# Expert rounds of 1792 columns in place of 896, in a two-layer hybrid decoder kernel

## The chip, the cores and the metric

The kernel runs on one NeuronCore of a Trainium2 chip. The metric is device time in microseconds (us) from launch to end, the median of several executions. TensorE (PE) multiplies, VectorE (DVE) and ScalarE (ACT) do the elementwise work, GpSimd (POOL) small index work, and SyncE (SP) issues nearly all transfers from device memory.

## The reference

The program is a two-layer decoder trunk on 256 tokens of width 1024, in float32. The part that the change touches is the last one, the expert feed-forward of the second layer:

```python
def moe_swiglu(h, router, we_gate, we_up, we_down):
    logits = (h @ router).astype(jnp.float32)
    top_v, top_i = lax.top_k(logits, TOP_K)
    top_w = jax.nn.softmax(top_v, axis=-1)
    gates = jnp.sum(jax.nn.one_hot(top_i, N_EXPERTS, dtype=jnp.float32) * top_w[..., None], axis=-2)
    gates = gates.astype(h.dtype)
    out = jnp.zeros_like(h)
    for e in range(N_EXPERTS):
        out = out + gates[..., e:e + 1] * swiglu(h, we_gate[e], we_up[e], we_down[e])
    return out
```

There are 8 experts, each token goes to 2 of them, and an expert's matrices are 1024x3584 (gate and up) and 3584x1024 (down): 44 MB an expert, 352 MB in all.

## The kernel before

Ahead of the experts stand the convolution layer, a dense feed-forward and the attention layer. They take the first 470 us or so and the change leaves their instructions as they are.

The experts are taken in an order that is worked out on the chip: those with more than 64 tokens alternate with the others, which keeps heavy and light experts next to each other. An expert's first 64 tokens go through `gate_up` and `down`. Up to 32 more, the overflow, go through `gate_up_over` and `down_over`, each inside an If on the register `over` (`over_parts`), so that PE jumps over them in an expert without overflow.

An expert is cut into `NR` rounds of `RW` columns of the hidden width; before, there are 4 rounds of 896. In a round PE does, in an order written out by hand (the loop over `rounds`, under `manual_schedule` for PE): `gate_up` of the first four blocks of 128 input rows; the transposes of the hidden values of the round before (`hidden_T`); if an expert has just ended, its `scatter` (the product with the tokens' placement matrix, which DVE then weighs and adds to `h`); in an expert's last round the `gather` of the next expert's tokens; overflow; `gate_up` of the other four blocks; overflow; and the seven `down` blocks of the round behind it. ACT and DVE make the hidden values from PSUM (`hidden`, `hidden_over`) while PE does those downs.

PSUM has eight banks of 512 columns. Before, `pa` and `pb` hold gate (upper 64 partitions) and up (lower 64), `po` the overflow, `py0` and `py1` the expert's output, and the three others turn (`bank`) among transposes, gather and scatter. The scatter splits the output into two float32r parts, `yh` and `yl`, and makes two products for each quarter of `h`.

Weights come through a ring of 19 tiles (`RING`, `raw_tile`) that SP fills in the order of use (`units`, `fetch`); SP issues a load when the readers of the tile 19 places earlier are done.

Of the kernel before, what the change touches and what calls it, by code (L numbers as in the profile page):

```python
# [17 lines left out]
P = 128  # L18
S = 256
# [28 lines left out]
def hybrid_kernel(  # L48
# [118 lines left out]
    with ExitStack() as ph:  # L167
# [189 lines left out]
        rows1 = consts.tile([P, P], F32, name="rows1")  # L357
# [303 lines left out]
    with ExitStack() as ph:  # L661
# [21 lines left out]
        def unit(v, src, how="(k p) n -> p k n"):  # L683
            sp.dma_start(v, src.rearrange(how, p=P))
            return v
# [11 lines left out]
        def units():  # L697

            for i in range(len(rounds) + 1):
                if i < len(rounds):  # L700
                    e, p = rounds[i]
                    for q in range(4):
                        for w in (sw_we_gate, sw_we_up):
                            t = raw_tile()[:, :2 * RW].rearrange("p (k n) -> p k n", k=2)
                            yield unit(t, matrix(w, e)[q * 256:(q + 1) * 256, p * RW:(p + 1) * RW])
                if i:
                    e, p = rounds[i - 1]
                    for q in range(4):
                        n = min(2, BLK - 2 * q)
                        t = raw_tile()[:, :n * D].rearrange("p (k n) -> p k n", k=n)  # L710
                        r0 = p * RW + 2 * q * P

                        yield unit(t, matrix(sw_we_down, e)[r0:r0 + n * P, :], "(p k) n -> p k n")
# [105 lines left out]
        pt = psm.enter_context(tc.tile_pool(name="pt", bufs=3, space=PSUM, reuse_waits="tile"))  # L819
        mwk = ga.enter_context(tc.tile_pool(name="mwk2", bufs=1, reuse_waits="tile"))  # L820

        def bank(name):
            return pt.tile([P, 512], F32, name=name, tag="t")

        def fixed(name):
            return pfix.tile([P, 512], F32, name=name)

        pa, pb, po = fixed("pa"), fixed("pb"), fixed("po")
        py = [fixed(f"py{n}") for n in range(2)]

# [70 lines left out]
        def gather(e, Pm):  # L901

            xe = wk.tile([P, KD, SL], F32, name="xe", tag="xe")
            for kk in range(2):
                b = bank("ga")[:, :4 * SL].rearrange("p (k n) -> p k n", k=4)
# [6 lines left out]
            b = bank("pmt")  # L912
# [3 lines left out]
            PT = wk.tile([P, 2, S], F32R, name="PT", tag="PT")  # L916
# [3 lines left out]
        def gate_up(xe, w, ks):  # L920
            for k in ks:
                x = xe[:, k, 0:HD]
                g, u = [v[:, k % 2, :] for v in w[2 * (k // 2):2 * (k // 2) + 2]]
                for ps, c0, c1 in ((pa, 0, A), (pb, A, RW)):
                    for half, v in ((0, g), (1, u)):
                        pe.matmul(ps[half * HD:(half + 1) * HD, :c1 - c0], x, v[:, c0:c1], start=(k == 0),  # L926
                                  stop=(k == KD - 1), tile_position=(0, half * HD))

        def gate_up_over(xe, w, ks):
            for k in ks:  # L930
                x = xe[:, k, HD:SL]
                for half, v in enumerate(w[2 * (k // 2):2 * (k // 2) + 2]):
                    for q, c0, c1 in ((2 * half, 0, A), (2 * half + 1, A, RW)):
                        pe.matmul(po[q * 32:(q + 1) * 32, :c1 - c0], x, v[:, k % 2, c0:c1], start=(k == 0),  # L934
                                  stop=(k == KD - 1), tile_position=(0, q * 32))

        def hidden():

            s = mwk.tile([P, A], F32, name="s", tag="s")
            hx = mwk.tile([P, A], F32, name="hx", tag="hx")  # L940
            act.activation(s[:HD, :], pa[:HD, :], AF.Silu)  # L941
            dve.tensor_tensor(hx[:HD, :], s[:HD, :], pa[HD:, :], op=OP.mult)  # L942
            act.activation(s[HD:, :B], pb[:HD, :B], AF.Silu)
            dve.tensor_tensor(hx[HD:, :2 * P], s[HD:, :2 * P], pb[HD:, :2 * P], op=OP.mult)
            dve.tensor_tensor(hx[HD:, 2 * P::2], s[HD:, 2 * P:B], pb[HD:, 2 * P:B], op=OP.mult)
# [7 lines left out]
        def hidden_over():  # L953
            s = mwk.tile([P, A], F32, name="so", tag="so")
            hx = mwk.tile([HD, A], F32, name="hxo", tag="hxo")
            act.activation(s[HD:, :B], po[:HD, :B], AF.Silu)
            act.activation(s[HD:HD + 32, B:], po[:32, B:], AF.Silu)  # L957
            dve.tensor_tensor(hx[:, :2 * P], s[HD:, :2 * P], po[HD:, :2 * P], op=OP.mult)  # L958
            dve.tensor_tensor(hx[:32, 2 * P:], s[HD:HD + 32, 2 * P:], po[HD:HD + 32, 2 * P:], op=OP.mult)
            dve.tensor_tensor(hx[32:, 2 * P::2], s[HD + 32:, 2 * P:B], po[HD + 32:, 2 * P:B], op=OP.mult)  # L960
            return hx

        def hidden_T(hx, hxo):
            b = bank("ht")
            for j in range(3):
                pe.transpose(b[:, j * P:(j + 1) * P], hx[:, hidden_block(j)], ident)
            pe.transpose(b[:, 3 * P:3 * P + HD], hx[:HD, hidden_block(3)], ident[:HD, :HD])  # L967
            hT = mwk.tile([P, 3 * P + HD], F32, name="hT", tag="hT")
            act.copy(hT, b[:, :3 * P + HD])  # L969
            b = bank("hto")  # L970
            for j in range(3):
                pe.transpose(b[:, j * HD:(j + 1) * HD], hxo[:, hidden_block(j)], ident[:HD, :HD])
            pe.transpose(b[:, 3 * HD:3 * HD + 32], hxo[:32, hidden_block(3)], ident[:32, :32])  # L973
            hTo = mwk.tile([P, 3 * HD + 32], F32, name="hTo", tag="hTo")
            dve.tensor_copy(hTo, b[:, :3 * HD + 32])  # L975
            return hT, hTo

        def down(p, hT, w):
            for q in range(BLK):
                o = q * P if q < 4 else (q - 4) * P + HD  # L980
                for n in range(2):
                    pe.matmul(py[n][n * HD:(n + 1) * HD, :], hT[:, o:o + HD], w[q // 2][:, q % 2, n * 512:(n + 1) * 512],  # L982
                              start=(p == 0 and q == 0), stop=(p == NR - 1 and q == BLK - 1),
                              tile_position=(0, n * HD))

        def down_over(p, hTo, w):
            for q in range(BLK):
                o = q * HD if q < 4 else (q - 4) * HD + 32
                i = p * BLK + q
                for n in range(2):  # L990
                    r = (HD, 0)[n] + 32 * (i % 2)
                    pe.matmul(py[n][r:r + 32, :], hTo[:, o:o + 32], w[q // 2][:, q % 2, n * 512:(n + 1) * 512],  # L992
                              start=(i < 2), stop=(i >= NR * BLK - 2), tile_position=(0, r))

        def outputs():
            ys = []
            for n in range(2):
                yh = mwk.tile([P, 512], F32R, name="yh", tag=f"yh{n}", bufs=1)
                yl = mwk.tile([P, 512], F32R, name="yl", tag=f"yl{n}", bufs=1)
                act.copy(yh, py[n])  # L1000
                dve.tensor_tensor(yl, py[n], yh.bitcast(F32), op=OP.subtract)  # L1001
                ys.append((yh, yl))
            return ys
# [167 lines left out]
```

## Time and profile before

| what | value |
|---|---|
| median of 3 runs | 1351.79 us (1348.92 to 1353.38) |
| profiled execution, its own time | 1349.67 us |
| its span, first to last instruction | 1348.0 us |
| PE busy, share of the span | 1282.6 us, 95% |
| DVE, ACT, POOL busy | 385.7, 298.9, 86.2 us |
| moved by the transfer queues | 420.91 MB, mean 312 GB/s |
| mean granted PE clock | 0.983 of full |

The profiled execution lies 2.1 us under the median of the runs, and 1.7 us of its time lie outside the span. A busy PE row means that matmuls follow each other; how close that is to the engine's best is seen from the spacing of their starts.

### The profile page before, as it was taken

How to read it: one execution, taken by the hardware profiler on the slowest of the kernel's cores; microseconds unless marked ns; L12 is line 12 of the kernel's file. 1: busy time of each engine (PE TensorE's matmuls, PEld its weight loads, DVE VectorE, ACT ScalarE, POOL GpSimd, SP SyncE). 2: the span in 40 equal slices, each digit the busy share in tenths (PEclk: the TensorE clock that was granted, in tenths of full speed). 3: DMA queues.
4: the chain of work that ended last, by engine and by line, in shares of the span. 5: the costliest groups of instructions: out<-in, count | busy, mean ns of one | idle time of the engine just before them, and what ended most of it. 6: DMA issues, size and time to landing. Idle time of an engine off the chain costs nothing. (4 is left out here: it accounts for less than half of the span.)

```text
span 1348.0 us, 19743 instructions
## 1 busy us (share of the span) xinstructions
PE 1282.6 (95%) x7908; PEld 721.9 (54%) x7908; DVE 385.7 (29%) x782; ACT 298.9 (22%) x575; POOL 86.2 (6%) x134
## 2 busy tenths in 40 slices
PE   6998899999889789999999999999999999999997
PEld 6854799999766533433544343454343454434443
DVE  5643554444576410102112011212011211200212
ACT  5444344444456110001001001111001010000111
POOL 4442000000030200000000000000000000000000
PEclk9999999999899889999999999999999999999999
DMA  8960265555370758899999999999999999999994
GB/s 283 318 169 26 70 213 187 188 188 188 99 245 28 299 208 313 342 346 413 409 409 409 411 409 403 409 412 409 409 409 406 410 408 410 412 409 408 403 412 192
DMA packets 137733, 420.91 MB, mean 312 GB/s; under 512 B 12250, under 2 KB 42776, under 8 KB 125336
## 3 DMA queue, kind: packets, MB, share of 16 engines
q1 hardware_dynamic: 133016, 414.39, 80.0%
q0 software_dynamic: 3456, 3.58, 1.2%
q8 instruction: 77, 1.26, 0.4%
q10 hardware_dynamic: 1152, 1.42, 0.3%
q14 instruction: 32, 0.26, 0.1%
HBM read 417.37 MB, written 1.95 MB: 311 GB/s over the span
## 5 line engine op out<-in xcount | busy, mean ns | idle before, releaser
L926 PE MATMUL pa<-raw,xe 128*64 128x512 f32 x1024 | 270.6, 599 | 6.6 <-DVE hx L942 4.0
L926 PE MATMUL pb<-raw,xe 128*64 128x384 f32 x1024 | 214.0, 488 | 0.0
L982 PE MATMUL py<-raw,hT 128*64 128x512 f32 x896 | 199.3, 595 | 4.0 <-PEq L1023 2.2
L926 PEld LDWEIGHTS pb<-raw,xe 128*64 128x64 f32 x1024 | 81.8, 138 | 139.6 <-issue 138.4
L91 DVE TENSOR_TENSOR wlo<-raw,whi 128x1024 fp32r<-128x1024 f32 x108 | 130.0, 1242 | 69.1 <-ACT whi L90 68.7
L982 PEld LDWEIGHTS py<-raw,hT 128*64 128x64 f32 x896 | 67.5, 137 | 131.9 <-issue 121.5
L926 PEld LDWEIGHTS pa<-raw,xe 128*64 128x64 f32 x1024 | 78.0, 137 | 104.1 <-issue 75.3
L90 ACT CAST whi<-raw 128x1024 fp32r<-128x1024 f32 x112 | 111.6, 1048 | 55.4 <-issue 24.5
L934 PE MATMUL po<-raw,xe 128*32 128x512 f32 (+1 forms) x1024 | 116.3, 542 | 0.0
L975 DVE COPY hTo<-hto 128x224 f32<-128x224 f32 x32 | 12.5, 391 | 353.7 <-PE hto L973 353.7
L969 ACT COPY hT<-ht 128x448 f32<-128x448 f32 x32 | 17.0, 532 | 374.8 <-PE ht L967 374.8
L934 PEld LDWEIGHTS po<-raw,xe 128*32 128x32 f32 x1024 | 43.8, 109 | 55.2 <-issue 43.2
L992 PE MATMUL py<-raw,hTo 128*32 128x512 f32 x448 | 64.5, 594 | 3.3 <-PEq L1023 3.3
L942 DVE TENSOR_TENSOR hx<-s,pa 64x512 f32<-64x512 f32 x32 | 22.1, 690 | 152.5 <-ACT s L941 152.2
L958 DVE TENSOR_TENSOR hxo<-so,po 64x256 f32<-64x256 f32 x32 | 13.5, 423 | 156.9 <-ACT so L957 156.6
L941 ACT ACTIVATE s<-pa 64x512 f32<-64x512 f32 x32 | 18.9, 590 | 164.4 <-PE pa L926 164.1
L98 PE MATMUL fg<-xh,whi 128*128 128x256 f32 x176 | 50.2, 286 | 2.7 <-ACT fsg L557 2.5
L98 PE MATMUL fu<-xh,whi 128*128 128x256 f32 x176 | 50.1, 284 | 0.0
L99 PE MATMUL fu<-xh,wlo 128*128 128x256 f32 x176 | 50.1, 284 | 0.0
L100 PE MATMUL fg<-xl,whi 128*128 128x256 f32 x176 | 50.0, 284 | 0.0
L99 PE MATMUL fg<-xh,wlo 128*128 128x256 f32 x176 | 50.0, 284 | 0.0
L100 PE MATMUL fu<-xl,whi 128*128 128x256 f32 x176 | 49.9, 284 | 0.0
(298 smaller groups left out, 1634.2 us busy)
## 6 DMA issues: line engine op xcount, KB each, us to landing
raw<-in_sw_we_gate_dram SPq DMA_DIRECT2D x128, 896.0 KB
raw<-in_sw_we_up_dram SPq DMA_DIRECT2D x128, 896.0 KB
raw<-in_sw_we_down_dram SPq DMA_DIRECT2D x96, 1024.0 KB
raw<-in_sw_we_down_dram SPq DMA_DIRECT2D x32, 512.0 KB
raw<-in_cv_w_gate_dram SPq DMA_DIRECT2D x11, 1024.0 KB
raw<-in_cv_w_up_dram SPq DMA_DIRECT2D x11, 1024.0 KB
raw<-in_cv_w_down_dram SPq DMA_DIRECT2D x11, 1024.0 KB
raw<-in_cv_w_in_dram SPq DMA_DIRECT2D x7, 1024.0 KB
```

The source lines that it names most:

```text
L90: act.copy(hi[:, i:i + step], v[:, i:i + step])
L91: (low or dve).tensor_tensor(lo[:, i:i + step], v[:, i:i + step], hi[:, i:i + step].bitcast(F32), op=OP.subtract)
L98: pe.matmul(ps, ah, bh, start=first, stop=False)
L99: pe.matmul(ps, al, bh, start=False, stop=False)
L100: pe.matmul(ps, ah, bl, start=False, stop=last)
L926: pe.matmul(ps[half * HD:(half + 1) * HD, :c1 - c0], x, v[:, c0:c1], start=(k == 0), stop=(k == KD - 1), tile_position=(0, half * HD))
L934: pe.matmul(po[q * 32:(q + 1) * 32, :c1 - c0], x, v[:, k % 2, c0:c1], start=(k == 0), stop=(k == KD - 1), tile_position=(0, q * 32))
L941: act.activation(s[:HD, :], pa[:HD, :], AF.Silu)
L942: dve.tensor_tensor(hx[:HD, :], s[:HD, :], pa[HD:, :], op=OP.mult)
L969: act.copy(hT, b[:, :3 * P + HD])
L982: pe.matmul(py[n][n * HD:(n + 1) * HD, :], hT[:, o:o + HD], w[q // 2][:, q % 2, n * 512:(n + 1) * 512], start=(p == 0 and q == 0), stop=(p ...
L992: pe.matmul(py[n][r:r + 32, :], hTo[:, o:o + 32], w[q // 2][:, q % 2, n * 512:(n + 1) * 512], start=(i < 2), stop=(i >= NR * BLK - 2), til ...
```

## The change

An expert now has two rounds of 1792 columns. A load of gate or up is one block of 128 rows by 1792 columns (7168 bytes a row; before, two blocks of 896 columns, 3584 bytes a row), the same 896 KB. Loads of gate, up and down are interleaved in the order of use, and a round's work is cut into four parts: two blocks of gate and up, their overflow, and up to four down blocks of the round behind.

Gate and up of 1792 columns need four banks, which are one tile, `pg`. `po` becomes one tile of two banks, and the three turning banks are gone: the transposes, gather and scatter write to `po`. The scatter takes the output in plain float32, one product for each quarter. The core of the diff:

```diff
-        RW = 896
+        RW = 1792
         NR = FE // RW
-        A, B = 512, 384
+        A, B = 1024, 768
...
+                for k in range(KD):
+                    if i < len(rounds):
+                        e, p = rounds[i]
                         for w in (sw_we_gate, sw_we_up):
+                            t = raw_tile()[:, :RW]
+                            sp.dma_start(t, matrix(w, e)[k * P:(k + 1) * P, p * RW:(p + 1) * RW])
+                            yield t
...
-        pa, pb, po = fixed("pa"), fixed("pb"), fixed("po")
-        py = [fixed(f"py{n}") for n in range(2)]
+        pg = pfix.tile([P, 4, 512], F32, name="pg")
+        po = pfix.tile([P, 2, 512], F32, name="po")
+        py = [pfix.tile([P, 512], F32, name=f"py{n}") for n in range(2)]
...
+            for b in range(2):
+                s = mwk.tile([P, 512], F32, name="s", tag="s")
+                n = (512, B - 512)[b]
+                act.activation(s[:HD, :], pg[:HD, b, :], AF.Silu)
+                dve.tensor_tensor(hx[:HD, b * 512:(b + 1) * 512], s[:HD, :], pg[HD:, b, :], op=OP.mult)
+                act.activation(s[HD:, :n], pg[:HD, 2 + b, :n], AF.Silu)
+                dve.tensor_tensor(hx[HD:, b * 512:b * 512 + n], s[HD:, :n], pg[HD:, 2 + b, :n], op=OP.mult)
...
         def outputs():
+            y = mwk.tile([P, 2, 512], F32, name="y", tag="y")
+            act.copy(y[:, 0, :], py[0])
+            dve.tensor_copy(y[:, 1, :], py[1])
+            return y
...
         def scatter(e, ys, PT):
             for n in range(2):
                 for t in range(2):
-                    b = bank("sc")
-                    for i in range(2):
-                        pe.matmul(b, PT[:, n, t * P:(t + 1) * P], ys[n][i], start=(i == 0), stop=(i == 1))
+                    b = po[:, t, :]
+                    pe.matmul(b, PT[:, n, t * P:(t + 1) * P], ys[:, n, :], start=True, stop=True)
...
+                for k in range(0, KD, 2):
...
+                    ms = range(2 * k, min(2 * k + 4, BLK))
+                    if not last_round:
+                        gate_up(xe[e][0], wgu, range(k, k + 1))
+                    if k == 0 and prev is not None:
+                        hT = hidden_T(prev[2])
+                    if not last_round:
+                        gate_up(xe[e][0], wgu, range(k + 1, k + 2))
+                    if k == 0:
+                        if prev is not None:
+                            hTo = hidden_over_T(prev[3])
...
+                    if k == KD - 2 and not last_round:
+                        hx = hidden()
+                    over_parts(None if last_round else (e, xe[e][0], wgu, range(k, k + 2)),
+                               None if prev is None else (prev[0], prev[1], hTo, wd, ms))
+                    if prev is not None:
+                        down(prev[1], hT, wd, ms)
```

Three places in the built program show how instructions move. A wait is given by the engine whose count it looks at.

The first is PE at the end of a round. Before, all the downs of the round behind (L982) stand between the last `gate_up` and the next one (L926); of those 14 the last six stand here:

```order
L982 MATMUL py_4455<-raw,hT 64x512 [waits DMAHW3_49]
L982 MATMUL py_4456<-raw,hT 64x512
L982 MATMUL py_4455<-raw,hT 64x512
L982 MATMUL py_4456<-raw,hT 64x512
L982 MATMUL py_4455<-raw,hT 64x512 [waits DMAHW4_49]
L982 MATMUL py_4456<-raw,hT 64x512
L926 MATMUL pa<-raw,xe 64x512 [waits DMAHW5_49,DVE_49]
L926 MATMUL pa<-raw,xe 64x512 [waits DMAHW6_49]
L926 MATMUL pb<-raw,xe 64x384 [waits DVE_49,Activation_49]
```

In the changed kernel only the last two of the 14 down blocks (L996) stand there, and one wait on DVE guards all four banks of `pg`:

```order
L996 MATMUL py_4451<-raw,hT 64x512 [waits DMAHW1_49]
L996 MATMUL py_4452<-raw,hT 64x512
L996 MATMUL py_4451<-raw,hT 64x512
L996 MATMUL py_4452<-raw,hT 64x512
L917 MATMUL pg<-raw,xe 64x512 [waits DMAHW3_49,DVE_49]
L917 MATMUL pg<-raw,xe 64x512 [waits DMAHW5_49]
L917 MATMUL pg<-raw,xe 64x512 x4
L917 MATMUL pg<-raw,xe 64x256 x2
```

Twelve of the fourteen blocks have moved ahead of the last `gate_up` of the round, and the count that the new wait names is that of the last of the four multiplications of `hidden`.

The second is PE where one expert is scattered and the next gathered. Before, the products (L1010) and the gather (L909, not in these rows) go to turning banks:

```order
L973 MATMUL hto<-ident,hxo 128x32
L1010 MATMUL sc<-yh,PT 128x512 [waits Activation_49]
L1010 MATMUL sc<-yl,PT 128x512 [waits DVE_49]
L1010 MATMUL sc<-yh,PT 128x512 [waits Activation_49]
L1010 MATMUL sc<-yl,PT 128x512
L1010 MATMUL sc<-yh,PT 128x512 [waits DVE_49]
L1010 MATMUL sc<-yl,PT 128x512
L1010 MATMUL sc<-yh,PT 128x512 [waits DVE_49]
L1010 MATMUL sc<-yl,PT 128x512
```

In the changed kernel all of it goes to `po`:

```order
L981 MATMUL po<-ident,hxo 128x32 x2
L1019 MATMUL po<-y,PT 128x512 [waits DVE_49] x4
L900 MATMUL po<-Pm_5357,hn 128x96 [waits DVE_49]
L900 MATMUL po<-Pm_5357,hn 128x96 x7
L900 MATMUL po<-Pm_5357,hn 128x96 [waits DVE_49]
L900 MATMUL po<-Pm_5357,hn 128x96 x7
L906 MATMUL po<-ident,Pm_5357 128x128 [waits Activation_49]
```

Each of the four products now waits for DVE's instruction that reads the product (or the transposes) before it, and each half of the gather for the read before that; the two banks of `po` do not alternate.

The third is DVE at the end of an expert. Before, the last multiplications of `hidden` stand ahead of the instructions that read `py` (L1001):

```order
L942 TENSOR_TENSOR hx<-s,pa 64x512 [waits Activation_49]
L944 TENSOR_TENSOR hx<-s,pb 64x256 [waits Activation_49]
L945 TENSOR_TENSOR hx<-s,pb 64x128
L1023 UNCONDITIONAL_BRANCH
L1001 TENSOR_TENSOR yl<-py_4455,yh 128x512 [waits Activation_49]
```

In the changed kernel the copy of `py` (L1012) stands between the first and the second multiplication of `hidden` (L937, L939):

```order
L937 TENSOR_TENSOR hx<-s,pg 64x512 [waits DVE_49,Activation_49]
L1012 COPY y<-py_4452 128x512 [waits PE_49]
L939 TENSOR_TENSOR hx<-s,pg 64x512 [waits Activation_49]
L937 TENSOR_TENSOR hx<-s,pg 64x512 [waits Activation_49]
L939 TENSOR_TENSOR hx<-s,pg 64x256 [waits Activation_49]
L954 TENSOR_TENSOR hxo<-so,po 64x512 [waits Activation_49]
```

The copy has moved into `hidden`, and it waits for the last down of the ending expert, which PE does after the last `gate_up`. The waits on ACT mean that ACT and DVE go in turns through `pg`.

## Rows read from the trace of the kernel before

**Rows 1.** Windows: stretch, length, each engine's busy us (instructions), clock, DMA share, GB/s.

```profile
480.00:1340.00 860.00, 845.22 (x4962) 362.27 (x4958) 127.48 (x300) 87.42 (x191) 0.00 (x0) 1.00 0.98 390
600.00:1300.00 700.00, 691.15 (x4042) 299.79 (x4040) 107.96 (x251) 71.35 (x157) 0.00 (x0) 1.00 1.02 408
```

**Rows 2.** Groups of PE, 480 to 1340 us: busy, mean ns, idle before, releasers.

```profile
L926 PE MATMUL pa<-raw,xe 128*64 128x512 f32 x1012 | 267.5, 599 | 6.6 <-DVE hx L942 4.0 <-PEq L1023 0.5
L982 PE MATMUL py<-raw,hT 128*64 128x512 f32 x896 | 199.3, 595 | 4.0 <-PEq L1023 2.2 <-DMA raw<-in_sw_we_gate_dram 0.8
```

**Rows 3.** Timeline, the end of a round without overflow (start, us, engine).

```profile
1280.78 1.06 PE L926 MATMUL pa<-raw,xe 128*64 128x512 f32 x4
1281.64 0.84 PE L926 MATMUL pb<-raw,xe 128*64 128x384 f32 x4
1281.92 0.59 ACT L941 ACTIVATE s<-pa 64x512 f32<-64x512 f32 x1 [8.02 <-PE pa L926]
...
1282.55 0.69 DVE L942 TENSOR_TENSOR hx<-s,pa 64x512 f32<-64x512 f32 x1 [5.25 <-ACT s L941]
1282.63 6.23 PE L982 MATMUL py<-raw,hT 128*64 128x512 f32 x28
...
1288.66 1.06 PE L926 MATMUL pa<-raw,xe 128*64 128x512 f32 x4
```

**Rows 4.** Packets of two short stretches: 914 to 928 us, then 906 to 910 us.

```profile
DMA packets 1677, 5.68 MB, mean 406 GB/s; under 512 B 100, under 2 KB 100, under 8 KB 1676
...
DMA packets 233, 1.69 MB, mean 423 GB/s; under 512 B 23, under 2 KB 23, under 8 KB 29
```

**Rows 5.** Groups of DVE and ACT, 480 to 1340 us.

```profile
L942 DVE TENSOR_TENSOR hx<-s,pa 64x512 f32<-64x512 f32 x32 | 22.1, 690 | 152.5 <-ACT s L941 152.2
L1012 DVE SCALAR_TENSOR_TENSOR h<-sc,G,h 128x512 f32<-128x512 f32 x29 | 19.8, 745 | 1.9 <-PE sc L1010 1.9
L941 ACT ACTIVATE s<-pa 64x512 f32<-64x512 f32 x32 | 18.9, 590 | 164.4 <-PE pa L926 164.1
...
L943 ACT ACTIVATE s<-pb 64x384 f32<-64x384 f32 x32 | 15.4, 482 | 0.8
...
L944 DVE TENSOR_TENSOR hx<-s,pb 64x256 f32<-64x256 f32 x32 | 13.6, 425 | 1.0
...
L975 DVE COPY hTo<-hto 128x224 f32<-128x224 f32 x32 | 12.5, 391 | 353.7 <-PE hto L973 353.7
...
L911 DVE COPY xe<-ga 128x384 f32<-128x384 f32 x7 | 3.9, 558 | 10.9 <-PE ga L909 10.9
```

**Rows 6.** Timeline of PE, the scatter of the first expert.

```profile
627.42 0.50 PE L1010 MATMUL sc<-yh,PT 128*128 128x512 f32 x1
...
629.88 1.08 PE L926 MATMUL pa<-raw,xe 128*64 128x512 f32 x4
```

**Rows 7.** Timeline of PE behind two Ifs (two places), and behind one (the third).

```profile
610.29 3.63 PE L992 MATMUL py<-raw,hTo 128*32 128x512 f32 x28 [0.84 <-PEq L1023]
...
708.34 6.23 PE L982 MATMUL py<-raw,hT 128*64 128x512 f32 x28 [0.43 <-DMA raw<-in_sw_we_gate_dram]
...
1331.23 6.23 PE L982 MATMUL py<-raw,hT 128*64 128x512 f32 x28 [0.30 <-PEq L1023]
```

**Rows 8.** Timeline, the end of the first round: PE waits for `hidden`.

```profile
498.64 1.98 PE L926 MATMUL pa<-raw,xe 128*64 128x512 f32 x4 [4.02 <-DVE hx L942]
...
504.24 1.02 PE L926 MATMUL pa<-raw,xe 128*64 128x512 f32 x4
```

**Rows 9.** Windows of the same place (columns as in the first group).

```profile
498.00:500.00 2.00, 1.36 (x4) 0.54 (x6) 1.22 (x3) 0.00 (x0) 0.00 (x0) 0.50 1.03 419
...
504.00:506.00 2.00, 2.00 (x14) 0.76 (x12) 0.00 (x0) 0.00 (x0) 0.00 (x0) 1.00 0.00 0
```

**Rows 10.** Timeline of the end: the last expert's output.

```profile
1337.46 1.08 ACT L1000 CAST yh<-py 128x512 fp32r<-128x512 f32 x2 [6.50 <-PE py L982]
...
1339.36 2.73 DVE L1012 SCALAR_TENSOR_TENSOR h<-sc,G,h 128x512 f32<-128x512 f32 x4
```

More of the change, by code (lines that the diff above doesn't have):

```diff
@@ L922, in gate_up @@
                 x = xe[:, k, 0:HD]
[L923 to L927, printed above, removed]
+                for b in range(4):
+                    c0, c1 = b * 512, min((b + 1) * 512, RW)
+                    for half in range(2):
+                        pe.matmul(pg[half * HD:(half + 1) * HD, b, :c1 - c0], x, w[2 * k + half][:, c0:c1],
+                                  start=(k == 0), stop=(k == KD - 1), tile_position=(0, half * HD))
         def gate_up_over(xe, w, ks):
@@ new lines, in hidden_over, with hidden_T @@
+            return hx
+        NB2 = B // P
+        BLA = A // P
+        def hidden_T(hx):
+            for j in range(BLA):
+                if j < NB2:
+                    pe.transpose(po[:, j // 4, j % 4 * P:j % 4 * P + P], hx[:, hidden_block(j)], ident)
+                else:
+                    o = NB2 % 4 * P + (j - NB2) * HD
+                    pe.transpose(po[:, 1, o:o + HD], hx[:HD, hidden_block(j)], ident[:HD, :HD])
+            hT = mwk.tile([P, BLK * HD], F32, name="hT", tag="hT")
+            act.copy(hT[:, :512], po[:, 0, :])
+            dve.tensor_copy(hT[:, 512:], po[:, 1, :BLK * HD - 512])
+            return hT
@@ new lines, in hidden_over_T @@
+        def hidden_over_T(hxo):
+            for j in range(BLA):
+                if j < NB2:
+                    pe.transpose(po[:, 0, j * HD:(j + 1) * HD], hxo[:, hidden_block(j)], ident[:HD, :HD])
+                else:
+                    o = NB2 * HD + (j - NB2) * 32
+                    pe.transpose(po[:, 0, o:o + 32], hxo[:32, hidden_block(j)], ident[:32, :32])
+            hTo = mwk.tile([P, BLK * 32], F32, name="hTo", tag="hTo")
+            dve.tensor_copy(hTo, po[:, 0, :BLK * 32])
+            return hTo
@@ L981, in down, with block_at @@
+        def block_at(m, n):
+            if m >= BLA:
+                return (m - BLA) * 2 * n + n
+            return m * 2 * n if m < NB2 else NB2 * 2 * n + (m - NB2) * n
+        def down(p, hT, w, ms):
+            for m in ms:
+                o = block_at(m, HD)
                 for n in range(2):
-                    pe.matmul(py[n][n * HD:(n + 1) * HD, :], hT[:, o:o + HD], w[q // 2][:, q % 2, n * 512:(n + 1) * 512],
-                              start=(p == 0 and q == 0), stop=(p == NR - 1 and q == BLK - 1),
+                    pe.matmul(py[n][n * HD:(n + 1) * HD, :], hT[:, o:o + HD], w[m // 2][:, m % 2, n * 512:(n + 1) * 512],
+                              start=(p == 0 and m == 0), stop=(p == NR - 1 and m == BLK - 1),
@@ L984, in down, with down_over @@
                               tile_position=(0, n * HD))
[L986 to L989, printed above, removed]
+        def down_over(p, hTo, w, ms):
+            for m in ms:
+                o = block_at(m, 32)
+                i = p * BLK + m
                 for n in range(2):
                     r = (HD, 0)[n] + 32 * (i % 2)
-                    pe.matmul(py[n][r:r + 32, :], hTo[:, o:o + 32], w[q // 2][:, q % 2, n * 512:(n + 1) * 512],
+                    pe.matmul(py[n][r:r + 32, :], hTo[:, o:o + 32], w[m // 2][:, m % 2, n * 512:(n + 1) * 512],
@@ L1035, in hybrid_kernel @@
                 last_round = i == len(rounds)
+                wgu, wd = [], []
                 if not last_round:
                     e, p = rounds[i]
-                    wgu = [ahead.pop(0) for _ in range(8)]
                     if p == NR - 1 and e + 1 < NE:
                         Pm = places(e + 1)
-                    gate_up(xe[e][0], wgu, range(4))
-                if prev is not None:
-                    wd = [ahead.pop(0) for _ in range(4)]
-                    hT, hTo = hidden_T(*prev[2:])
@@ L1045, in hybrid_kernel @@
-                if ys is not None:
-                    scatter(*ys)
-                    ys = None
-                if not last_round:
-                    if p == NR - 1 and e + 1 < NE:
-                        xe[e + 1] = gather(e + 1, Pm)
-                    over_parts((e, xe[e][0], wgu, range(4)), None)
-                    gate_up(xe[e][0], wgu, range(4, KD))
-                    hx = hidden()
-                over_parts(None if last_round else (e, xe[e][0], wgu, range(4, KD)),
-                           None if prev is None else (prev[0], prev[1], hTo, wd))
```

108 lines of the change are left out of this document (38 added, 70 removed).

## The prediction

> **What bounds the kernel now.** I first read windows over the expert part, to see which engine has room. From 480 to 1340 us PE is busy for 845.2 of 860 us, so it stands idle for 14.8; from 600 to 1300 us it is idle for 8.9 of 700, and in the same stretch the transfer engines show a share of 1.02 at 408 GB/s [rows 1]. Two things look full at once. To tell them apart I read what PE waits for: the largest waits are 4.0 us for DVE's `hx` and 2.2 for its own sequencer, and for a load it waits 0.8 us in the group of downs [rows 2]. Last I looked at whether the busy rows hide a slow engine: in a light round the `pa` group of four rows (gate and up, 512 columns) starts at 1280.78 and `pb` at 1281.64, 0.86 us later, and this spacing holds everywhere that I looked, in light and heavy rounds alike [rows 3]. PE never slows down for a load. The experts' 352.3 MB take 863 us at 408 GB/s, PE's work takes 845: the ring lets light experts lend their time to heavy ones, and both flows come out almost equal. So PE can win at most its 14.8 us from faster loads, and whatever makes PE wait is added in full.
>
> **Faster loads.** A stretch with loads of gate and up alone (3584-byte packets) moves 406 GB/s, one that is nearly all down (8192 bytes) 423 [rows 4]. By engine that is 141 and 310 ns a packet, so 7168 bytes are estimated at 272.5 ns, 421 GB/s. Gate and up are 256 loads of 917.5 KB, 234.9 MB: 579 us become 558, a gain of 21 us for the transfers. From below it is nothing, as the 8192-byte stretch is short and single windows in it go lower. For PE the gain is what it now waits for loads; I take 2 us.
>
> The Trainium skill ("DMA: Bandwidth & Descriptors", section on why small descriptors are slow) gives a fixed 3 cycles for each packet beside one for every 32 bytes; by it 3584 bytes lose 2.6% and 7168 lose 1.3%, so the gain would be about 8 us. The rows show it larger.
>
> **The end of a round.** Before, seven down blocks cover `hidden`: PE starts them at 1282.63 and the next `gate_up` follows at 1288.66, without a gap, though `hidden` begins at 1281.92 [rows 3]. After, two blocks stand there, 2 x 0.86 = 1.73 us, and the first matmul waits for the last of four multiplications, between which ACT and DVE take turns. ACT needs 0.59 us for 512 columns and, from 0.59 and 0.48 for 384, about 0.37 for 256; DVE 0.69 and 0.425 [rows 5]. A handover takes 0.04 (ACT ends at 1282.51, DVE starts at 1282.55) [rows 3], taken as 0.05. The chain is 3 x (0.59 + 0.69) + 0.37 + 0.425 + 8 x 0.05 = 5.05 us. Three cases follow. Four of the eight experts have overflow (every other one, the first included).
> - Second round of a light expert, three times with a round behind it: cover 1.73 and one If at 0.2 to 0.3 [rows 7], wait 3.1 us, 9.3 in all.
> - First round of experts 1 to 7: the copy of `py` stands on DVE behind the first multiplication and waits for the last down. When PE has done it, DVE still has the copy (0.69, from 391 ns for 224 columns and 558 for 384) and the rest of the chain: 0.05 + 0.69 + 0.69 + 0.05 + 0.59 + 0.05 + 0.69 + 0.05 + 0.37 + 0.05 + 0.425 + 0.05 = 3.75 us, whether there is overflow or not; 7 x 3.75 = 26.2.
> - Second round of a heavy expert: overflow covers it, 0. The first round of all waits 4.0 us already [rows 8]; unchanged.
>
> Sum 35.5 us. Behind the waiting matmul stands all of PE, and so the release of the ring's tiles.
>
> **Scatter.** Eight float32r products took from 627.42 to 629.88, 2.46 us [rows 6]. Four float32 products of 512 columns now go in turns with DVE. No row shows such a product at full width; the nearest is the `pa` group, whose two half-width products take 1.06 us from start to end [rows 3]. If the halves run side by side, a full product takes that too; if they run one behind the other, 0.43 less. I take 1.06, as four quarter-width overflow products also run together. With 0.745 for DVE [rows 5] and two handovers a quarter takes 1.9 us, four 7.6, or 5.15 more; seven times 36.1 us. Lower bound (0.63): 24.
>
> **Transposes and gather.** The copy of `hTo` (448 columns, 0.62 by the same two rows, and 0.1) stands before the scatter or gather of every second round and the overflow of three first rounds: 11 x 0.72 = 7.9. The transposes wait for `hidden_over`, 3.1 us behind `hidden`, under a `gate_up` block of 3.0: 0.1 each, 1.5. In the gather PE waits for the two copies, 0.56 and 0.48 [rows 5] with 0.1 each: 1.24 x 8 = 9.9; four times overflow then waits for `PT` (0.59 + 0.1): 2.7. Sum 22.0; half of it if buffered work overlaps better than I see.
>
> **Ifs.** Two Ifs cost 0.84 us where the first is jumped and 0.43 where the second is; one 0.30 [rows 7]. A light expert now has four pairs and four single Ifs (4.56; before one pair and seven, 2.94), a heavy one behind a light one four pairs (1.72 for 0.43): 4 x 1.6 + 3 x 1.3 = 10.3 us. Nothing, if the sequencer runs ahead.
>
> **The end.** After the last `gate_up` nothing covers `hidden` and `hidden_over` (5.05 + 3.1) but 1.73 us of downs and an If: PE waits 6.2, then 1.3 for the copies of `hT`. The last output took 4.6 us (1337.46 to 1342.09) [rows 10]; now 0.74 for `y` and 7.6, hence 3.8 more. Sum 11.3.
>
> **The clock.** Behind the wait of 4.02 us the clock shows 0.50 until it is back at 1.00 in the window at 504 [rows 9]: 1.2 GHz, then 2.4. From 498.64 to 504.24 stand four `pa` and `pb` groups that take 3.01 us at full clock; 2.6 are lost [rows 8]. The new waits of 3.1 to 6.2 us, eleven of them, may each cost this: 0 to 29 us. I take half, 14.
>
> The Trainium skill ("TensorE: Matmul & The Clock Gate", on how the gate oscillates in real kernels) says that a wait between bursts of matmuls brings the clock back to half, and the next burst begins cold. The trace agrees in this one place; by the page the term would be 29 rather than 14.
>
> **The sum.** 35.5 + 36.1 + 22.0 + 10.3 + 11.3 + 14 - 2 = 127.2. On the profiled execution's 1349.67 (2.1 under the median) that is 1477 us.
>
> **The rivals.**
> - The clock falls at every wait, and in the scatter too, where PE is busy about half of 7.6 us: 29 for 14, and 2.6 for each of seven scatters, 33 more: 1510. For it speaks the one wait that can be read; against, that shorter gaps may pass. 0.17.
> - Light experts swallow their waits: if loads in truth set the pace there, only heavy experts count. Light ones carry 4 x 3.75 + 9.3 at round ends, 4 x 5.15 of scatter, about 10 of transposes and gather and 6.4 of Ifs, 61 in all: 1416. For it speaks the transfer share of 1.02; against, the spacing of 0.86 in a light round, in which a load-bound PE would have gaps. 0.17.
> - Faster: loads set the pace throughout, and the longer packets pay. It decides where the new waits of PE stay under the 14.8 us that it now stands idle, so if the four banks of `pg` were freed one by one and the quarters of the scatter overlapped; then PE's floor is 845 of 860 us, and the time 1335. The built order speaks against it. 0.03.
> - The loads don't get faster: it changes nothing here but the 2 us, since PE sets the pace. No change within 0.3%, the least that a measurement of this kernel can tell, would need waits of under 4 us: 0.02.
>
> **How the numbers follow.** My forecast has 0.61. The bounds of its unknown terms (scatter 24 to 36, gather 11 to 22, Ifs 0 to 10, clock 0 to 29) give 1430 to 1492; with the two rivals of the same sign the range is 1412 to 1515. Faster 0.03, same 0.02, slower 0.95.
>
> **What would show it.** In the profile after, PE's idle before `pg` should be some 36 us with DVE's `hx` as releaser, in waits of 3 to 4 us; before the scatter's matmuls some 20 to 25 us with DVE `h` as releaser; before the gather some 10. The transfer share should drop to about 0.9, and SP should wait for PE. The clock should show 0.50 behind the longer waits. I am wrong if PE idles for loads, or if `gate_up` starts while `hidden` is still at the later banks of `pg`.

## The result, and the profile after

The change makes the kernel slower: **1511.44 us**, median of 5 runs (1509.54 to 1516.81), against 1351.79 before (1348.34 to 1353.38); the ratio is 1.1195, with an interval of 1.1174 to 1.1215. The profiled execution has a span of 1507.7 us, and PE is busy for 1350.4 of them, more than the whole span was before (1348.0).

First the windows over the expert part, which answer to [rows 1]:

```profile
480.00:1500.00 1020.00, 914.12 (x4992) 362.89 (x4991) 121.50 (x218) 79.17 (x153) 0.00 (x0) 0.94 0.81 330
600.00:1450.00 850.00, 760.71 (x4116) 304.77 (x4114) 102.01 (x180) 62.99 (x123) 0.00 (x0) 0.94 0.85 346
```

PE stands idle for 105.9 us where it was 14.8, and it is busy for 69 us longer. The clock tells most of why: 0.94 over the part instead of 1.00; the plain float32 products of the scatter are longer too (below). The transfer engines went from a share of 1.02 to 0.85, so loads don't set the pace. What PE waits for (the waits of PE, 470 to 1510 us: total, times, longest; [rows 2] before):

```profile
PE pg L917 <- DVE hx L939: 34.7, 11, 3.8
PE po L1019 <- DVE h L1021: 20.3, 24, 0.8
PE py L1006 <- PEq L1032: 10.1, 12, 0.9
PE po L966 <- DVE hxo L957: 6.1, 1, 6.1
PE po L900 <- DVE xe L902: 5.2, 8, 0.7
PE po L900 <- DVE h L1021: 5.1, 6, 0.8
PE po L1019 <- DVE hTo L983: 5.0, 7, 0.7
PE po L906 <- ACT xe L902: 4.6, 8, 0.6
```

The first line is the round ends; the others, but for the Ifs (`PEq`) and the end of the last expert (`L966`), are the two banks of `po`. Here is one round end, a light expert's first round, in the timeline (start, us, engine; [rows 3] before):

```profile
641.20 0.69 DVE L937 TENSOR_TENSOR hx<-s,pg 64x512 f32<-64x512 f32 x1 [37.33 <-ACT s L936]
641.92 0.59 ACT L938 ACTIVATE s<-pg 64x512 f32<-64x512 f32 x1 [0.76 <-DVE hx L937]
642.30 1.94 PE L996 MATMUL py<-raw,hT 128*64 128x512 f32 x8
644.27 0.58 ACT L1011 COPY y<-py 128x512 f32<-128x512 f32 x1 [1.76 <-PE py L996]
644.31 0.69 DVE L1012 COPY y<-py 128x512 f32<-128x512 f32 x1 [2.42 <-PE py L996]
645.03 0.69 DVE L939 TENSOR_TENSOR hx<-s,pg 64x512 f32<-64x512 f32 x1
...
647.51 0.42 DVE L939 TENSOR_TENSOR hx<-s,pg 64x256 f32<-64x256 f32 x1 [0.44 <-ACT s L938]
...
647.99 5.79 PE L917 MATMUL pg<-raw,xe 128*64 128x512 f32 x16 [3.75 <-DVE hx L939]
```

ACT and DVE take turns, and both copies of `y` stand in the middle of the chain, waiting for the last down. PE waits 3.75 us, and then its 16 rows take 5.79 us instead of the 3.2 that they take at full clock. The scatter, in the same expert's second round:

```profile
662.13 1.12 PE L1019 MATMUL po<-y,PT 128*128 128x512 f32 x2 [0.84 <-DVE h L1021]
663.30 0.75 DVE L1021 SCALAR_TENSOR_TENSOR h<-po,G,h 128x512 f32<-128x512 f32 x1 [1.22 <-PE po L1019]
664.10 1.12 PE L1019 MATMUL po<-y,PT 128*128 128x512 f32 x2 [0.84 <-DVE h L1021]
...
668.04 2.02 PE L900 MATMUL po<-Pm,hn 128*128 128x96 f32 x16 [0.84 <-DVE h L1021]
```

A quarter takes 1.97 us (0.84 of it waiting), four 7.9. In this passage the clock holds. In another it does not; the same lines of PE three experts on:

```profile
1036.38 1.12 PE L1019 MATMUL po<-y,PT 128*128 128x512 f32 x2 [0.72 <-DVE hTo L983]
1038.35 1.57 PE L1019 MATMUL po<-y,PT 128*128 128x512 f32 x2 [0.84 <-DVE h L1021]
1040.76 2.08 PE L1019 MATMUL po<-y,PT 128*128 128x512 f32 x2 [0.84 <-DVE h L1021]
...
1046.60 3.73 PE L900 MATMUL po<-Pm,hn 128*128 128x96 f32 x16 [0.84 <-DVE h L1021]
1050.98 3.73 PE L900 MATMUL po<-Pm,hn 128*128 128x96 f32 x16 [0.65 <-DVE xe L902]
```

Against the first passage, the products go from 1.12 to 2.08 and from 2.02 to 3.73 us while the waits between them stay as they were. The windows of that place (the clock is the third column from the end):

```profile
1040.00:1050.00 10.00, 7.55 (x20) 4.40 (x20) 2.21 (x3) 0.00 (x0) 0.00 (x0) 0.50 0.00 0
1050.00:1060.00 10.00, 8.11 (x40) 5.28 (x43) 1.47 (x5) 1.06 (x2) 0.00 (x0) 0.50 0.00 0
1060.00:1070.00 10.00, 10.00 (x58) 2.81 (x52) 0.00 (x0) 0.00 (x0) 0.00 (x0) 0.86 0.83 322
```

No wait in this passage is over 0.84 us, and yet the clock is at 1.2 GHz for more than 20 us. Over all windows of 5 us in the expert part I add up PE's busy time times what the clock lacks of 1.00: 49.9 us are lost to it, 26 of them in four of the seven passages of scatter and gather, 14 behind seven of the eleven round ends, the rest at the start and the end. Before, the same sum was 4.5. I call it the **clock loss** below; it is always that of the one profiled execution.

### The profile page after: what moved, and what is told of

Read it like the earlier page. It is cut to its first block, busy times and chain, and to the rows that moved or that the text cites. A ratio compares the mean times of both kernels' runs of the same rounds, so it can differ in the third digit from the quotient of the medians.

```text
span 1507.7 us, 19450 instructions
## 1 busy us (share of the span) xinstructions
PE 1350.4 (90%) x7908; PEld 724.1 (48%) x7908; DVE 379.0 (25%) x694; ACT 289.7 (19%) x535; POOL 86.2 (6%) x134
## 5 line engine op out<-in xcount | busy, mean ns | idle before, releaser
L917 PE MATMUL pg<-raw,xe 128*64 128x512 f32 (+1 forms) x2048 | 417.5, 558 | 34.7 <-DVE hx L939 34.7
L917 PEld LDWEIGHTS pg<-raw,xe 128*64 128x64 f32 x2048 | 160.2, 141 | 303.0 <-issue 246.0
L996 PE MATMUL py<-raw,hT 128*64 128x512 f32 x896 | 210.9, 609 | 5.6 <-PEq L1032 2.9
L937 DVE TENSOR_TENSOR hx<-s,pg 64x512 f32<-64x512 f32 x32 | 22.1, 690 | 630.3 <-ACT s L936 630.3
L936 ACT ACTIVATE s<-pg 64x512 f32<-64x512 f32 x32 | 18.9, 590 | 625.0 <-PE pg L917 317.1
L996 PEld LDWEIGHTS py<-raw,hT 128*64 128x64 f32 x896 | 66.6, 139 | 141.9 <-issue 132.5
L1019 PE MATMUL po<-y,PT 128*128 128x512 f32 x64 | 44.1, 777 | 25.9 <-DVE h L1021 20.3
L900 PE MATMUL po<-Pm,hn 128*128 128x96 f32 x256 | 46.0, 354 | 14.2 <-DVE xe L902 5.2
L900 PEld LDWEIGHTS po<-Pm,hn 128*128 128x128 f32 x256 | 42.8, 261 | 23.1 <-DVE h L1021 12.1
L1006 PEld LDWEIGHTS py<-raw,hTo 128*32 128x32 f32 x448 | 16.9, 109 | 41.5 <-issue 37.4
L98 PEld LDWEIGHTS fg<-xh,whi 128*128 128x128 f32 x176 | 34.9, 198 | 3.7 <-ACT fsg L557 2.7
```

The lines of the kernel that those rows point to most:

```text
L98: pe.matmul(ps, ah, bh, start=first, stop=False)
L917: pe.matmul(pg[half * HD:(half + 1) * HD, b, :c1 - c0], x, w[2 * k + half][:, c0:c1], start=(k == 0), stop=(k == KD - 1), tile_position=(0 ...
L937: dve.tensor_tensor(hx[:HD, b * 512:(b + 1) * 512], s[:HD, :], pg[HD:, b, :], op=OP.mult)
L1006: pe.matmul(py[n][r:r + 32, :], hTo[:, o:o + 32], w[m // 2][:, m % 2, n * 512:(n + 1) * 512], start=(i < 2), stop=(i >= NR * BLK - 2), til ...
L1019: pe.matmul(b, PT[:, n, t * P:(t + 1) * P], ys[:, n, :], start=True, stop=True)
```

## The experiments

Theory: two PSUM tiles that are waited for as a whole (`po`, `pg`) make the waits, and the waits make the cold clock, which costs about half as much again. Rivals: only the long waits at round ends cool the clock; the round of 1792 columns is the loss; the size of the loads matters. Each ratio stands against the kernel before, measured in the same series.

### Taking the two tiles apart, and holding back the copies of y

`po` as two tiles of a bank each; nothing else:

```diff
-        po = pfix.tile([P, 2, 512], F32, name="po")
+        po = [pfix.tile([P, 512], F32, name=f"po{b}") for b in range(2)]
```

> The two banks of po become two tiles, so a product of scatter or gather waits only for the DVE or ACT read of the bank that it writes itself; nothing else changes. My theory: the largest loss is the passage of scatter and gather, by its idle time (20.3 us before L1019 behind DVE's h, some 15 us more before the gather's and the transposes' products) and again by the clock, which stands at 0.50 for 10 to 25 us behind most of these passages. Then the idle time falls by 30 to 40 us, the time at half clock from 127 us to about 60, and the kernel takes 1430 to 1450 us. Rival 1, the clock falls because of the 3.75-us waits at the ends of rounds alone: the time at half clock stays over 100 us, and the kernel takes 1470 to 1480. Rival 2, the passage is set by something else (loads, ACT): 1500 or more.

Measured: 1440.84 us, ratio 1.0669 (1.0651 to 1.0686), 71 us less, as expected. The waits on `DVE h` and `xe` are gone and the passage runs through, in PE's timeline:

```profile
640.34 6.18 PE L917 MATMUL pg<-raw,xe 128*64 128x512 f32 x16 [3.75 <-DVE hx L939]
...
652.95 3.95 PE L1019 MATMUL po<-y,PT 128*128 128x512 f32 x8 [0.77 <-DVE hTo L983]
656.89 3.81 PE L900 MATMUL po<-Pm,hn 128*128 128x96 f32 x32
```

Four quarters take 3.95 us instead of 7.9. The waits that went are 20.3 + 5.1 + 5.2 + 4.6 = 35.2 us, the clock loss fell from 49.9 to 19.6, and the waits of 3.75 us at round ends are all still there. The rival of the long waits falls.

`pg` as four tiles of a bank each, alone:

```diff
-        pg = pfix.tile([P, 4, 512], F32, name="pg")
+        pg = [pfix.tile([P, 512], F32, name=f"pg{b}") for b in range(4)]
...
-                for b in range(4):
+                for b in (0, 2, 1, 3):
```

> The four banks of pg become four tiles, and gate_up takes the banks in the order 0, 2, 1, 3 in which hidden reads them; nothing else changes. My theory: the next round's gate_up then starts while hidden is still at the later banks, and ends 1.6 us earlier at each of 11 round ends, since it still waits for the last multiplication but with one product pair left to do: 18 us less idle time (the 34.7 us before pg become 15 to 20, in more and shorter waits), and some clock comes back: 1475 to 1495 us. Rival 1, only long waits lower the clock, and all cold time is theirs: 1440 to 1460. Rival 2, the wait for hidden was not on the path that sets the end, since loads would have come later anyway: 1505 or more.

Measured: 1485.03 us (1476 to 1494), ratio 1.0976 (1.0908 to 1.1044). The time was right, the reason was not. All 34.7 us before `pg` are gone, not half: in the trace ACT's second activation no longer waits for DVE's first multiplication, `hidden` begins bank by bank, and both copies of `y` now come after it. But the kernel gained only 26 us, and the profiled execution, at 1491.87 us one of the two long ones, only 18, since its clock loss went up, to 78.2. The scatter of the same expert, in PE's timeline:

```profile
642.54 3.18 PE L917 MATMUL pg<-raw,xe 128*64 128x512 f32 x16
...
654.38 2.07 PE L1019 MATMUL po<-y,PT 128*128 128x512 f32 x2 [0.84 <-DVE h L1021]
657.30 2.08 PE L1019 MATMUL po<-y,PT 128*128 128x512 f32 x2 [0.84 <-DVE h L1021]
```

No wait over 0.84 us stands ahead of it in this expert, and the passage is cold; in this run all seven are. Why some stay warm in the changed kernel is not settled. The clock is not fixed by the kernel alone: the four executions with this split took 1476 to 1494 us, at mean granted clocks of 0.938 to 0.923.

Then the copies of `y`. First both are issued only behind DVE's last multiplication of `hidden`, which in the built order moved DVE's copy alone; then behind ACT's last activation as well (`ends` holds the two instructions), as in this diff:

```diff
-            act.copy(y[:, 0, :], py[0])
-            dve.tensor_copy(y[:, 1, :], py[1])
+            with ExitStack() as pins:
+                for ins in ends:
+                    pins.enter_context(tc.issue_after(ins))
+                act.copy(y[:, 0, :], py[0])
+                dve.tensor_copy(y[:, 1, :], py[1])
```

> The copies of the output y are held back on ACT and DVE until the last multiplication of hidden has been issued, so that the copy of DVE no longer stands inside the chain of hidden; nothing else changes. My theory: the first rounds of the three heavy experts behind another are covered by their overflow and lose their 3.75-us wait altogether, those of the four light ones go from 3.75 to about 3.1: 13 to 14 us of idle time less, the clock gives up to 8 more: 1488 to 1500 us. Rival 1, the wait is the chain of hidden itself, whatever stands between: no change, 1508 to 1515. Rival 2, the later copy delays hidden_over and the scatter: slower by 3 to 10 us.

Measured with DVE's alone: 1512.06 us, ratio 1.1208 (1.117 to 1.1246), no change; a miss, at the time of the first rival but not for its reason. The four waits of 3.75 us fell to 2.7, 4.0 us in all, while the clock loss was 58.5 in place of 49.9. ACT's copy was still in the chain, as this heavy expert's round end shows:

```profile
764.83 0.69 DVE L941 TENSOR_TENSOR hx<-s,pg 64x512 f32<-64x512 f32 x1 [0.65 <-ACT s L940]
...
768.46 0.58 ACT L1017 COPY y<-py 128x512 f32<-128x512 f32 x1 [3.66 <-PE py L999]
768.94 0.59 ACT L938 ACTIVATE s<-pg 64x512 f32<-64x512 f32 x1
```

ACT has nothing to do for 3.66 us, because the copy stands ahead of the next activation.

> As the changed kernel, but both copies of y, ACT's and DVE's, are held back behind the last activation and the last multiplication of hidden; the run that held back DVE's alone moved nothing, and its trace shows ACT's copy still standing in the middle of the chain, waiting for the last down. My theory: it was this copy. Now the first rounds of the three later heavy experts are covered by their 3.6 us of overflow and lose their wait, those of the four light experts fall to about 1.3 us, the second rounds of light ones keep 2.9: the 34.7 us before pg become 15 to 20, the time 1485 to 1500 us. Rival, the chain itself is the wait: no change again, 1508 to 1515.

Measured with both: 1491.12 us, ratio 1.0992 (1.0931 to 1.1053). The waits before `pg` are 16.4 us in 8: none at the first rounds of the three later heavy experts, 1.06 to 1.27 at the light ones, 2.93 at second rounds, 2.77 at the first round of all. The clock loss, 56.2, did not fall: four passages are cold again, not the same four. So the prediction's mechanism was right in kind; it had seen one of the two copies.

### Work that only keeps PE busy

One unneeded product behind each quarter of the scatter (`warm` is set for all but the last), and the same behind each half of the gather:

```diff
+                    if warm:
+                        pe.matmul(py[0][:, :256], ident, hn[:, 0, :256], start=True, stop=True)
                     hs = h[:, t, n * 512:(n + 1) * 512]
                     dve.scalar_tensor_tensor(hs, b, G2[:, t, e:e + 1], hs, op0=OP.mult, op1=OP.add)
```

> PE gets one product more behind each quarter of the scatter and behind each half of the gather (float32, 256 columns, about 0.56 us, into a py bank that nobody reads then): work that the kernel does not need, put where PE now waits 0.7 to 0.85 us. Nothing else changes. My theory: PE then counts as busy in these passages, the clock stays up behind them, and the 60 to 70 us that now follow them at 0.50 go back to 1.00: 25 to 35 us come back though work was added: 1475 to 1490 us. Rival 1, the clock falls for another reason (the 3.75-us waits, or the passage's products as such): the time at half clock stays at about 127 us and the time stays or grows by up to 10 us: 1510 to 1522.

Measured: 1474.29 us, ratio 1.0915 (1.0897 to 1.0934): 37 us come back though PE has more to do, a little more than the expected 25 to 35. The passage in PE's timeline, and its waits at round ends:

```profile
653.19 1.13 PE L1020 MATMUL po<-y,PT 128*128 128x512 f32 x2 [0.41 <-DVE h L1024]
654.15 0.60 PE L1022 MATMUL py<-hn,ident 128*128 128x256 f32 x2
655.16 1.12 PE L1020 MATMUL po<-y,PT 128*128 128x512 f32 x2 [0.41 <-DVE h L1024]
...
659.10 2.02 PE L900 MATMUL po<-Pm,hn 128*128 128x96 f32 x16 [0.41 <-DVE h L1024]
...
PE pg L918 <- DVE hx L940: 34.4, 11, 3.8
```

A quarter still takes 1.97 us, and the long waits at round ends are still there, but the clock loss is 14.1 instead of 49.9. That gaps inside the passages cool the clock is thereby shown, not only argued: whether the gaps are taken out (`po` split) or filled, the clock stays up. The Trainium skill ("TensorE: Matmul & The Clock Gate", section "A second HAM failure mode: psum-queue depth-cycling") describes a kernel in which PE stops briefly and often between groups of products into PSUM, and the clock swings; the trace agrees, at gaps of 0.84 us.

### The same fault in the kernel before

The kernel before, four rounds of 896 columns, with one turning bank in place of three:

```diff
-        pt = psm.enter_context(tc.tile_pool(name="pt", bufs=3, space=PSUM, reuse_waits="tile"))
+        pt = psm.enter_context(tc.tile_pool(name="pt", bufs=1, space=PSUM, reuse_waits="tile"))
```

> The kernel before, with its four rounds of 896 columns, but one PSUM bank in place of the three that turn among transposes, gather and scatter, so that each product into it waits for the read of the one before; nothing else changes. My theory: the lost banks cost here too, about 60 us of waits (32 rounds at 0.65 for the transposes behind each other, 7 scatters at 3.4, 8 gathers at 1.2) and some of the clock: 1405 to 1460 us. Rival, the round of 1792 columns is what makes the banks scarce and slow, before has enough cover elsewhere: 1350 to 1370.

Measured: 1495.43 us, ratio 1.1058 (1.1024 to 1.1091): nearly the loss of the whole change, without the change. The waits came to 58 us, as expected; the clock loss, 81.6 us, was more than I allowed for. Its scatter in the timeline:

```profile
650.65 0.80 PE L1010 MATMUL sc<-yh,PT 128*128 128x512 f32 x1 [0.84 <-DVE h L1012]
...
656.16 1.98 PE L926 MATMUL pa<-raw,xe 128*64 128x512 f32 x4
657.89 1.53 PE L926 MATMUL pb<-raw,xe 128*64 128x384 f32 x4
```

The `pa` group behind the passage takes 1.98 us where [rows 3] has 1.06. With unneeded products in the gaps, those between the two sets of transposes of each round too:

> As the kernel before with one bank, plus one unneeded product (float32, 256 columns, 0.56 us, into a spare PSUM bank that nobody reads) behind the first transposes of each round, each quarter of the scatter and each half of the gather, where PE waits 0.5 to 0.9 us. The run without them came out 144 us above before, of which its trace shows 62 as waits and 184 us more at half clock. My theory: the other 80 us are the cold clock that short waits in close order bring about, and they come back: time at half clock under 60 us, 1410 to 1435 us. Rival, the clock is low for another reason, and the added products cost their own time: 1490 or more.

Measured: 1429.25 us, ratio 1.0571 (1.0553 to 1.0588), clock loss 10.0: 66 us back. In this kernel the cold clock costs more than the waits that bring it about, 77 us over the kernel before against 58.

### Both splits, and what is left

> Both splits at once: po as two tiles, pg as four with the banks taken in the order 0, 2, 1, 3. Measured alone, the first took 71 us off and the second 26, of which the second paid 25 to 30 back in longer half-clock time behind the passages of scatter and gather. My theory (waits on whole tiles and the cold clock behind them are the loss, the round of 1792 columns itself is not): the two together give more than their sum, since the passages now stay warm: no waits before pg and before the scatter's quarters, half-clock time about 30 us, 1380 to 1400 us. What then stands above before is the Ifs (13 us of idle time), the float32 scatter (about 15), the end and the copies of hTo (5 to 10 each). Rival, the gains overlap (the clock falls again at the few waits that are left): 1415 to 1425.

Measured: 1384.81 us, ratio 1.0246 (1.0226 to 1.0266). Of the 160 us, 127 are the two tiles; alone the splits gave 71 and 26, which is 97; together they give more, since the passages that the second leaves cold are warm with the first. Clock loss 6.9. Its window, to be read against [rows 1]:

```profile
600.00:1300.00 700.00, 674.37 (x3918) 271.17 (x3916) 92.35 (x164) 58.41 (x114) 0.00 (x0) 1.00 0.97 395
```

The largest waits of PE that are left:

```profile
PE py L1006 <- PEq L1032: 10.3, 12, 1.0
PE po L1019 <- DVE hTo L983: 5.4, 7, 0.8
PE py L996 <- PEq L1032: 3.6, 15, 0.5
```

Here PE is near [rows 1] again, so the loads should show their worth if they have one: the same with loads of 896 columns.

```diff
-                            sp.dma_start(t, matrix(w, e)[k * P:(k + 1) * P, p * RW:(p + 1) * RW])
+                            for c in range(0, RW, 896):
+                                sp.dma_start(t[:, c:c + 896], matrix(w, e)[k * P:(k + 1) * P, p * RW + c:p * RW + c + 896])
```

> As the run with both splits, but each load of gate and up in two of 896 columns (3584-byte packets, as before). My theory: PE sets the pace, so the longer packets are worth nothing; the transfer rate falls from about 420 to 406 GB/s, the time stays within 4 us of the run with both splits. Rival: now that PE waits less, loads are near the path, and the shorter packets cost 10 to 21 us.

Measured: 1386.87 us (1384.25 to 1387.14), ratio 1.0257 (1.0235 to 1.0279), the same within what the runs can tell. The packets of 700 to 760 us with the long loads:

```profile
DMA packets 3777, 25.17 MB, mean 419 GB/s; under 512 B 418, under 2 KB 418, under 8 KB 2748
```

The same stretch with the short ones:

```profile
DMA packets 6259, 24.63 MB, mean 411 GB/s; under 512 B 696, under 2 KB 696, under 8 KB 5248
```

Longer packets do move faster here, 419 against 411 GB/s, and it is worth nothing, since PE sets the pace: over 600 to 1300 us the two kernels move 395 and 396 GB/s.

Next a cheaper product in the scatter, one float32r instead of float32, on top of both splits (the placement matrix `PT` becomes float32r too):

```diff
-            y = mwk.tile([P, 2, 512], F32, name="y", tag="y")
+            y = mwk.tile([P, 2, 512], F32R, name="y", tag="y")
```

> As the run with both splits, but the expert's output and the placement matrix of the scatter are float32r, so each quarter is one product that rounds the output instead of a plain float32 one (the result loses digits; this only prices the product). My theory: eight passages of scatter go from 4.0 us of products to four of about 0.3 us each, held up by DVE's reads to about 2.2 us in all: 12 to 15 us less, 1369 to 1373 us. Rival, the passage is set by DVE or by what stands behind it: 1380 or more.

Measured: 1389.6 us, ratio 1.0278 (1.0261 to 1.0296): a miss, no faster than with both splits and by the medians 4.8 us slower. In PE's timeline:

```profile
643.03 0.74 PE L1019 MATMUL po<-y,PT 128*128 128x512 f32 x2 [0.77 <-DVE hTo L983]
644.38 1.45 PE L1019 MATMUL po<-y,PT 128*128 128x512 f32 x2 [0.61 <-DVE h L1021]
646.02 6.25 PE L900 MATMUL po<-Pm,hn 128*128 128x96 f32 x32 [0.19 <-DVE h L1021]
```

The scatter ends 1.0 us sooner (2.99 us from its first product to the gather, against 3.94), but PE now waits for DVE in it, the clock falls, and the gather takes 6.25 us instead of 3.81. Five of the seven passages of scatter and gather go this way, and the clock loss is 21.9 instead of 6.9. Whether the waits or the shorter products bring the clock down, no run separates.

Last the order of the two banks. Beginning each pair of the scatter's quarters with the second bank, and then the gather and its transposes with the second too:

```diff
-                for t in range(2):
+                for t in (1, 0):
...
-                b = po[kk][:, :4 * SL].rearrange("p (k n) -> p k n", k=4)
+                b = po[1 - kk][:, :4 * SL].rearrange("p (k n) -> p k n", k=4)
```

> As the run with both splits, but each pair of the scatter's quarters begins with the second bank of po instead of the first, which the transposes of the overflow have just written. My theory: the first product no longer waits 0.77 us for the copy of hTo, seven times: 5.4 us less idle time, 1377 to 1381 us. Rival, the last quarter is now in the bank that the gather begins with, so the gather waits instead: 1383 to 1386.

Measured with the scatter's order alone: 1384.3 us, ratio 1.0233 (1.0216 to 1.025). The rival was right: the 5.4 us before the scatter came back as this wait of the gather.

```profile
PE po L900 <- DVE h L1021: 5.1, 6, 0.8
```

> As the run in which the scatter begins with the second bank, whose trace shows the 5.4 us saved before the scatter coming back as 5.1 us before the gather (it began with the bank that the last quarter had just written). Now the gather begins with the second bank too, and so do the transposes behind it, so that the two banks strictly take turns through the whole passage. My theory: both waits are gone, 5 us less than with both splits: 1377 to 1381 us. Rival, the products then come upon the reads one place later (the transposes behind the gather, the overflow behind the placement matrix): 1383 to 1386 again.

Measured with both: 1376.05 us, ratio 1.0179 (1.0163 to 1.0195), just under the expected 1377 and the best version with the large rounds; it does not reach the kernel before. Against that, its trace keeps the Ifs (17.7 us of waits, before 6.8; how they are counted is said below) and a scatter of 3.96 us against 2.46 [rows 6], eight times 1.5; the rest are waits of 1 to 3 us for `hTo` and `hxo`.

## Why the prediction was right in kind and short in size

The forecast was 1477, the result 1511. That is above the 1492 to which the forecast's own terms could reach; it lies in the range because the range took in the first rival, at 1510. The waits that the prediction named are in the profile after, on the releasers that it named. Term by term, the forecast first and then what that profile shows:

- **Round ends**, forecast 35.5 us: 34.7 less the 4.0 that were there before, 30.7. The chain with the copy took 3.75 us as worked out, but four times, not seven: at three first rounds the copies stood one place later in the chain, and it took 2.7. I had named DVE's copy alone, and the runs show that ACT's must go too.
- **Scatter**, 36.1: a quarter 1.97 us for 1.9, the product 1.12 for 1.06; (7.9 - 2.46) x 7 = 38.
- **Transposes and gather**, 22.0: `hTo` 7.8 in all, the gather's copies 9.8, `PT` 2.7; 20.3.
- **Ifs**, 10.3: 16.3 us after, 6.8 before; 9.5. The waits on the sequencer are 13.0 of the 16.3. The other 3.3 the profile puts down to loads (2.5) and to `hTo` (0.8), but all sixteen places of light experts where the overflow's downs stand behind two Ifs wait 0.82 to 0.90 us, whichever releaser is named, as these two in PE's timeline; so I count them as Ifs:

```profile
604.04 1.92 PE L1006 MATMUL py<-raw,hTo 128*32 128x512 f32 x16 [0.82 <-DMA raw<-in_sw_we_gate_dram]
616.39 1.92 PE L1006 MATMUL py<-raw,hTo 128*32 128x512 f32 x16 [0.83 <-PEq L1032]
```

  Before, too, this place had the largest wait on the sequencer, which the prediction's list leaves out (it had the price, 0.84, from [rows 7]). PE's waits before:

```profile
PE py L992 <- PEq L1023: 3.3, 4, 0.8
```

- **The end**, 11.3: 6.1 and 1.3 as worked out, and the last output took 8.5 us (1494.25 to 1502.71) against the 4.6 of [rows 10]; 11.2.
- **Loads**, minus 2: 0. The 0.8 us before downs in [rows 2], from which this came, stand behind Ifs as well (one of them is the 0.43 of [rows 7]); before and after, PE has no wait that must be a load's, so there was nothing to gain.
- **The clock**, 14: measured 49.9 - 4.5 = 45. This is the step that failed. I priced it at the eleven long waits alone and took half of 29 us; the round ends lost 14, as taken, but the half was a guess: seven of the eleven are followed by a cold stretch. The passages of scatter and gather lost 26 more, which stood only in the rival, and the last round and the cold start some more.

The measured terms add up to 155 of the 159.7 us between the two spans; of the rest, 3 lie ahead of the experts (the first gather starts at 472.21 us, before at 469.01). The first rival had the places right, but its time came out of other parts: it put 2.6 us on each of eleven waits and seven scatters, 29 and 18 us, and what happened is fewer and, in the scatter, longer cold stretches, 14 and 26. That its sum lies within 2 us of the result is luck. Light experts did not swallow their waits: their round ends and scatter are in the trace at full length. The sentence that I would be wrong if `gate_up` started while `hidden` was at the later banks holds in the changed kernel, whose eleven waits all end with the last multiplication. The split of `pg` tested it: with the split `gate_up` does start early, and the waits vanish.

## What to carry to other kernels

In these kernels a PSUM tile of several banks is waited for as one; where products alternate with reads, a bank apiece, and taking them strictly in turns, gave back 135 of the 160 us. When PE has to wait often for less than a microsecond, price the passage twice: once for the waits, and once for the products in and behind it at half clock. A faster product on PE may gain nothing where the next engine then makes it wait, as the float32r scatter did not.

## What was not expected of the hardware

Gaps of 0.84 us between products of 1.12 us brought the clock to 0.50, for up to 25 us, and in the changed kernel did so in four of seven passages that look alike. Added products that nobody needs saved 37 us in one kernel and 66 in another. The program alone does not fix the clock: executions of one and the same kernel, that with `pg` split, lay up to 18 us apart, the longer ones at the lower mean clock.
